# RMSNorm and projection on one core: warm-up matmuls on a tile of their own, and the last two stores from two engines

## The chip, the cores and the metric

The kernel runs on one core of a Trainium2 chip. The metric is the device time of one execution in microseconds (us), as the median of several runs. The span is what the profile shows of such a run, from the first to the last instruction; it is 1.7 to 1.9 us shorter than the device time. TensorE does the matmuls, VectorE (DVE) and ScalarE (ACT) the elementwise work, GpSimd (POOL) little, SyncE (SP) issues transfers. PSUM is the memory that the matmuls write to; an eviction copies a result out of it.

## The reference

```python
def reference(x, gamma, w_qkv, eps):          # x: 8 x 1024 x 768, w_qkv: 768 x 2304, float32
    rms = np.sqrt(np.mean(x ** 2, axis=-1, keepdims=True) + eps)
    x_norm = x / rms * gamma
    return np.matmul(x_norm, w_qkv).astype(np.float32)
```

The 8192 rows are 64 row tiles of 128 rows. The 768 columns of x are six blocks of 128 (the sums of the matmul), and the 2304 output columns are stored as 1024, 1024 and 256.

## The kernel before

The weights are scaled by gamma and rounded to bfloat16 once. Of each row tile, x is cast, transposed (by TensorE for the first four, by a transposing transfer for the others), multiplied with the weights, and scaled by 1/rms when PSUM is evicted. A plan gives each instruction a time, and the instructions are emitted in that order. TensorE starts with matmuls that produce nothing of use, to bring its clock up while the first data arrive.

```python
    ones = nc.const_aps.tensor(1.0, [P, NT], bf16)        # one constant per partition, repeated 512 times
    g6 = singles.tile([KO, P], f32)
    nc.scalar.dma_start(out=g6, in_=gamma.rearrange("(ko p) -> ko p", p=P))
    eps_sb = singles.tile([P, 1], f32)
    nc.vector.memset(eps_sb, float(eps))
    # ... identity, g_sb, w_b (the weights), then the pools of x, of weights and of outputs

    def idle(n, nl=P):
        wps = psum.tile([P, NT], f32, name="pm")
        for _ in range(n):
            nc.tensor.matmul(out=wps[:, :nl], lhsT=ones[:, :P], rhs=ones[:, :nl], start=True, stop=True)

    def store(t, h, n0, nl):
        p0 = PARTS[h][0]
        nc.sync.dma_start(out=of[t * P:(t + 1) * P, n0:n0 + nl], in_=OUT[t, h][:, n0 - p0:n0 - p0 + nl])

    def width(t, n0):             # the last row tile ends in two pieces of 128 columns
        return P if t == MT - 1 and n0 >= N - 2 * P else min(NT, N - n0)
    # ...
    at(0.0, idle, 5, NT)          # five warm-up matmuls
    at(2.8, gamma_in)             # gamma is transposed
    at(2.81, idle, 6, NT)         # six more, then the transposes of the first x tile
```

## Time and profile before

| what | value |
|---|---|
| device time, median of the first 3 runs | 388.34 us (388.09 to 388.74) |
| span of the profiled run | 386.9 us |
| TensorE busy | 98% of the span |
| warm-up matmuls on the constants | 14, 5.4 us busy |
| start of the last matmul to the end of the span | 3.88 us |

A line of the timeline reads: start, duration, engine, source line, operation, result and operands, shape and count; in brackets the idle time of the engine before it and what ended that. `PEld` is TensorE's weight load, `SPq` and `ACTq` are issues of transfers. The lines that carry the argument stand in the prediction below.

### The profile page before, as it was taken

Reading aid. Unit: us, or ns where it says so; the run is one execution under the profiler, and the core shown is the slowest. Engines: PE = TensorE matmul, PEld = TensorE weight load, DVE = VectorE, ACT = ScalarE, POOL = GpSimd, SP = SyncE. Lnnn points to the kernel's source line nnn. Section 1 sums busy time; section 2 is a strip of 40 time slices with the busy share of each in tenths; the row PEclk is TensorE's granted clock in tenths of the full one; section 3 lists DMA queues with packets and bytes.
Section 4 is the critical chain, followed back from the end, with each engine's and each line's share of the span. In section 5 each row is a group of like instructions: output and inputs, shape, how many; then the busy total and the mean of one; then the engine's idle time right before and its main releaser. Section 6 shows DMA issues by size and latency. Waiting matters only on the chain.

```text
span 386.9 us, 5470 instructions
## 1 busy us (share of the span) xinstructions
PE 379.9 (98%) x1927; PEld 192.2 (50%) x1965; DVE 153.4 (40%) x307; ACT 181.6 (47%) x365; POOL 6.5 (2%) x14
## 2 busy tenths in 40 slices
PE   8999999999999999999999999999999999999996
PEld 4444655454554554554554554554554554554553
DVE  2744534434333344333344333343333343333332
ACT  4752644453544443544444444544444534434532
POOL 0130000000000000000000000000000000000000
PEclk9999999999999999999999999999999999999999
DMA  8999999999999999999999999999999999999985
GB/s 291 390 281 402 398 318 363 344 338 283 351 297 308 303 295 321 293 300 322 305 289 313 285 318 312 293 309 275 326 311 297 304 317 305 304 306 289 292 264 186
DMA packets 89719, 119.91 MB, mean 310 GB/s; under 512 B 52438, under 2 KB 61532, under 8 KB 89692
## 3 DMA queue, kind: packets, MB, share of 16 engines
q1 hardware_dynamic: 89680, 119.56, 101.2%
q8 instruction: 15, 0.25, 0.3%
q14 instruction: 12, 0.10, 0.1%
q10 hardware_dynamic: 12, 0.00, 0.0%
HBM read 32.25 MB, written 75.50 MB: 279 GB/s over the span
## 4 chain that ended last, share of the span: by engine, by line
PE 89%; DMA 8%; issue 1%; DVE 1%; ACT 1%; SPq 0%
PE pm L235 89%; DMA x_t<-in_x_dram 3%; DMA w_f<-in_w_qkv_dram 2%; DMA xT<-xb 2%; DMA out_dram<-ot 1%; ACT ot L251 1%; DVE ot L249 0%; DVE xb L174 0%; SPq L160 0%; SPq L155 0%; SPq L255 0%; ACT w_b L168 0%
## 5 line engine op out<-in xcount | busy, mean ns | idle before, releaser
L235 PE MATMUL pm<-w_b,xT 128*128 128x512 bf16 (+1 forms) x1888 | 372.1, 357 | 2.1
L235 PEld LDWEIGHTS <-xT 128*128 128x128 bf16 x1926 | 187.9, 98 | 185.5 <-DMA xT<-xb 0.5
L249 DVE TENSOR_SCALAR ot<-pm,rstd 128x512 f32<-128x512 f32 (+1 forms) x161 | 111.5, 695 | 206.1 <-PE pm L235 201.7
L251 ACT ACTIVATE ot<-pm,rstd 128x512 f32<-128x512 f32 (+2 forms) x160 | 102.7, 643 | 191.7 <-PE pm L235 151.0
L185 ACT ACTIVATE sq<-x_t 128x768 bf16<-128x768 f32 x64 | 53.4, 834 | 3.0 <-DMA x_t<-in_x_dram 3.0
L174 DVE CAST xb<-x_t 128x768 bf16<-128x768 f32 x61 | 33.2, 545 | 13.6 <-DMA x_t<-in_x_dram 13.5
L187 ACT ACTIVATE rms<-ssq,eps_sb 128x1 f32<-128x1 f32 x64 | 18.8, 294 | 2.1
L185 ACT ACTIVATION_READ_ACCUMULATOR sq<-x_t 128x1 f32 x64 | 12.2, 191 | 0.0
L166 DVE TENSOR_SCALAR w_b<-w_f,g_sb 128x512 bf16<-128x512 f32 (+1 forms) x16 | 7.7, 499 | 5.9 <-DMA w_f<-in_w_qkv_dram 5.9
L192 DVE RECIPROCAL rstd<-rms 128x1 f32<-128x1 f32 x64 | 9.8, 153 | 0.0
L170 POOL TENSOR_SCALAR w_b<-w_f,g_sb 128x512 bf16<-128x512 f32 (+1 forms) x8 | 5.8, 735 | 23.5 <-DMA w_f<-in_w_qkv_dram 23.5
L284 PE MATMUL pm<-const-bfloat16-1.0 128*128 128x512 bf16 (+1 forms) x14 | 5.4, 539 | 0.8 <-PEq L340 0.8
L168 ACT ACTIVATE w_b<-w_f,g_sb 128x512 bf16<-128x512 f32 (+1 forms) x6 | 3.6, 612 | 2.7 <-DMA w_f<-in_w_qkv_dram 2.7
L212 PE MATMUL pm<-ident_f,x_t 128*128 128x128 f32 x18 | 2.8, 300 | 0.3 <-DMA x_t<-in_x_dram 0.3
L212 PEld LDWEIGHTS pm<-ident_f,x_t 128*128 128x128 f32 x18 | 2.4, 160 | 1.3 <-DMA x_t<-in_x_dram 0.9
L284 PEld LDWEIGHTS <-const-bfloat16-1.0 128*128 128x128 bf16 x14 | 1.5, 126 | 2.7 <-issue 2.7
L176 ACT CAST xT<-pm 128x256 bf16<-128x256 f32 (+1 forms) x5 | 2.3, 458 | 0.9 <-PE pm L212 0.7
L142 ACT ACT_TABLE_LOAD x1 | 1.3, 1283 | 1.4 <-PEq L340 1.4
L174 DVE CAST xT<-pm 128x512 bf16<-128x512 f32 x1 | 0.7, 691 | 1.4 <-PE pm L212 1.4
L267 DVE COPY g_sb<-pm 128x6 f32<-128x6 f32 x1 | 0.2, 164 | 1.9 <-PE pm L266 1.9
L266 PEld LDWEIGHTS pm<-ident_f,g 6*128 6x128 f32 x1 | 0.2, 177 | 1.0 <-issue 1.0
L174 DVE COPY xT<-pm 128x768 bf16<-128x768 bf16 x1 | 0.6, 557 | 0.0
(12 smaller groups left out, 2.5 us busy)
## 6 DMA issues: line engine op xcount, KB each, us to landing
out_dram<-ot SPq DMA_DIRECT2D x124, 512.0 KB, 3.9
x_t<-in_x_dram SPq DMA_DIRECT2D x64, 384.0 KB, 4.2
out_dram<-ot SPq DMA_DIRECT2D x63, 128.0 KB, 3.2
w_f<-in_w_qkv_dram SPq DMA_DIRECT2D x10, 512.0 KB, 7.4
out_dram<-ot SPq DMA_DIRECT2D x8, 256.0 KB, 2.0
w_f<-in_w_qkv_dram SPq DMA_DIRECT2D x4, 256.0 KB, 6.6
xT<-xb SPq DMA_TRANSPOSE x60, 4.3
w_f<-in_w_qkv_dram SPq DMA_DIRECT2D x2, 384.0 KB, 6.1
```

The source lines that it names most:

```text
L166: nc.vector.tensor_scalar(out=o, in0=i, scalar1=g, scalar2=None, op0=mult)
L168: nc.scalar.activation(out=o, in_=i, func=AF.Copy, scale=g, bias=0.0)
L170: nc.gpsimd.tensor_scalar(out=o, in0=i, scalar1=g, scalar2=1.0, op0=mult, op1=mult)
L174: nc.vector.tensor_copy(out=out, in_=in_)
L185: nc.scalar.activation(out=sq, in_=X[t], func=AF.Square, accum_out=ssq)
L187: nc.scalar.activation(out=rms, in_=ssq, func=AF.Sqrt, scale=inv_k, bias=eps_sb)
L192: nc.vector.reciprocal(out=r, in_=RS[t])
L212: nc.tensor.transpose(out=PT[t, h][:, ko - k0, :], in_=X[t][:, ko * P:(ko + 1) * P], identity=ident_f)
L235: nc.tensor.matmul(out=PM[t, n0][:, :nl], lhsT=XT[t][:, ko, :], rhs=w_b[:, ko, n0:n0 + nl], start=(b == 1), stop=(b == KO))
L249: nc.vector.tensor_scalar(out=o, in0=pm[:, :nl], scalar1=RS[t], scalar2=None, op0=mult)
L251: nc.scalar.activation(out=o, in_=pm[:, :nl], func=AF.Copy, scale=RS[t], bias=0.0)
L284: nc.tensor.matmul(out=wps[:, :nl], lhsT=ones[:, :P], rhs=ones[:, :nl], start=True, stop=True)
```

## The change

The warm-up gets a tile of its own in place of the program's constants; VectorE must write it first, and one warm-up matmul is given up for that time. At the end the second-to-last store is issued by ScalarE, so that the last one need not queue behind it on SyncE.

```diff
-    ones = nc.const_aps.tensor(1.0, [P, NT], bf16)
+    ones = singles.tile([P, NT], bf16)
+    nc.vector.memset(ones, 1.0)
...
     def store(t, h, n0, nl):
         p0 = PARTS[h][0]
-        nc.sync.dma_start(out=of[...], in_=OUT[t, h][...])
+        queue = nc.scalar if t == MT - 1 and n0 == N - 2 * P else nc.sync
+        queue.dma_start(out=of[...], in_=OUT[t, h][...])
...
-    at(0.0, idle, 5, NT)
+    at(0.0, idle, 4, NT)
```

More of the change, by code (lines that the diff above doesn't have):

```diff
@@ L254, in store @@
         p0 = PARTS[h][0]
-        nc.sync.dma_start(out=of[t * P:(t + 1) * P, n0:n0 + nl], in_=OUT[t, h][:, n0 - p0:n0 - p0 + nl])
+        queue = nc.scalar if t == MT - 1 and n0 == N - 2 * P else nc.sync
+        queue.dma_start(out=of[t * P:(t + 1) * P, n0:n0 + nl], in_=OUT[t, h][:, n0 - p0:n0 - p0 + nl])
     plan = []
```

## The prediction

> **What bounds the kernel now.** I read the page first: busy time by engine, the groups of instructions, the chain that ended last. Then the timeline of the first 14 us, the timeline of the last 4 us in narrow windows, and the DMA activity of those last microseconds, because the change touches only the two ends.
>
> ```profile
> PE 379.9 (98%) x1927; PEld 192.2 (50%) x1965; DVE 153.4 (40%) x307; ACT 181.6 (47%) x365; POOL 6.5 (2%) x14
> L235 PE MATMUL pm<-w_b,xT 128*128 128x512 bf16 (+1 forms) x1888 | 372.1, 357 | 2.1
> L284 PE MATMUL pm<-const-bfloat16-1.0 128*128 128x512 bf16 (+1 forms) x14 | 5.4, 539 | 0.8 <-PEq L340 0.8
> ```
>
> TensorE is busy 98% of the 386.9 us span, and its 1888 real matmuls sat idle only 2.1 us in all. That work is untouched, so the change can act only on the microseconds before the real work runs back to back and on the microseconds after the last matmul. The warm-up matmuls of the third line are what the first part edits.
>
> The start, from the timeline (start, duration, engine, line):
>
> ```profile
> 0.78 2.29 PE L284 MATMUL pm<-const-bfloat16-1.0 128*128 128x512 bf16 x5 [0.78 <-PEq L340]
> 0.81 0.06 DVE L139 MEMSET eps_sb<- 128x1 f32 x1 [0.81 <-PEq L340]
> 3.18 0.18 PEld L266 LDWEIGHTS pm<-ident_f,g 6*128 6x128 f32 x1 [1.02 <-issue]
> 3.38 2.74 PE L284 MATMUL pm<-const-bfloat16-1.0 128*128 128x512 bf16 x6
> 5.52 0.20 PEld L212 LDWEIGHTS pm<-ident_f,x_t 128*128 128x128 f32 x1 [0.31 <-DMA x_t<-in_x_dram]
> 5.91 1.14 PE L212 MATMUL pm<-ident_f,x_t 128*128 128x128 f32 x6
> 7.38 0.88 PE L212 MATMUL pm<-ident_f,x_t 128*128 128x128 f32 x6 [0.32 <-DMA x_t<-in_x_dram]
> ```
>
> The reader is to see two joints. TensorE runs five warm-up matmuls, the transpose of gamma, six more, then the transposes of the first x tile; and there is a gap at 7.38 us, where it waits 0.32 us for the second x tile from memory. From that tile on it runs almost without a gap. The gap is slack: whatever delays TensorE by less than about 0.3 us before it costs nothing.
>
> The end, from four narrow windows of the timeline, joined by dots:
>
> ```profile
> 382.56 1.02 DVE L249 TENSOR_SCALAR ot<-pm,rstd 128x512 f32<-128x512 f32 x2 [1.84 <-DMA out_dram<-ot]
> 382.90 0.37 ACT L251 ACTIVATE ot<-pm,rstd 128x128 f32<-128x128 f32 x1 [0.94 <-PE pm L235]
> 383.34 0.33 SPq L255 DMA_DIRECT2D out_dram<-ot  x1
> ...
> 383.77 0.88 SPq L255 DMA_DIRECT2D out_dram<-ot  x2
> ...
> 384.24 0.40 SPq L255 DMA_DIRECT2D out_dram<-ot  x1
> ```
>
> The last three stores stand in one queue on SyncE: the 256 KB one at 383.34, the second-to-last (64 KB, out of ScalarE's eviction) at 383.77, the last (64 KB, out of VectorE's) at 384.24. Both small evictions are done by 383.27 and 383.58, so the last store waits 0.66 us for its turn, not for data. It lands 1.6 us after its issue, and the span ends at 386.9.
>
> **What the Trainium skill says.** (1) "VectorE: DVE Perf Modes", section "Zero memsets can be issued as uint32 (trn2)": a memset takes one cycle per element whatever the dtype; the page's specification table gives 0.96 GHz. No memset of 512 elements is in the trace of before (the one of 1 element took 0.06 us), so nothing confirms it yet. (2) "TensorE: Matmul & The Clock Gate", "Part 1: The HAM clock gate": matmuls run at half clock until about 3.4 us of sustained activity has been seen in a window that runs freely. The trace agrees on the half clock, not on so short a wait: warm-up matmuls start 0.427 us apart, the first x tile's transposes 0.21 us apart up to 6.5 us, the second x tile's 0.11 us apart. The doubling falls near 6.6 us, 5.8 us after the first matmul. The profile's own clock row shows full clock throughout; the spacing decides. (3) "DMA: Bandwidth & Descriptors", "Issuing engines are not separate DMA queues": transfers issued from two engines run on the same 16 DMA engines, and only issue time is saved. The trace shows such issue time: 383.34 to 383.77 to 384.24 is 0.43 and 0.47 us a step.
>
> **The change part by part.** I also compared the instruction order of the two kernels on each engine. It changes in four places only: VectorE gets one memset, first of all; TensorE loses one warm-up load and matmul (the first group is 4, not 5) and its first load waits for VectorE; SyncE loses the second-to-last store; ScalarE gets it as its last instruction. All else stays in order.
>
> Start. The memset should last 512 / 0.96 GHz + 0.06 = 0.59 us (an estimate by page (1) and the small memset's 0.06 us). It starts at 0.81 and ends at 1.40; with 0.05 us for the semaphore (chosen from hand-overs elsewhere in the trace) the first matmul starts near 1.48 in place of 0.78: +0.70 us. One matmul fewer takes back 0.427. So the gamma transpose is at most 0.27 us later, and less if it waits for gamma's transfer: that one's last packets move between 2.6 and 2.8 us, and a wait event stands at 3.1. The x transposes then start at 5.91 to 6.18, and six of them at the cold 0.21 us spacing occupy TensorE until at most 6.18 + 1.28 = 7.46, against the 7.38 where the second tile arrives. If the clock doubles at 6.6 as before they are done by 7.0. Loss: 0.0 to 0.1 us. The moment of doubling can itself move later, as activity starts 0.7 us later; transposes and matmuls after 7.38 that are still cold cost half of the cold time, and I allow 0.1 us on average. VectorE's identity cast and eps move by up to 0.6 us; the cast's first reader comes at 11.98, the scaled weights wait for a transfer at 4.62: hidden. Sum of the start: +0.1 us.
>
> End. SyncE issues the 256 KB store at 383.34 and then the last store at 383.77 in place of 384.24: 0.47 us earlier. ScalarE issues the second-to-last at about 383.3, right after its own eviction. If nothing else limited, the end would move by 0.47. But the three transfers share the 16 engines: from the first data packet at 384.14 to the last near 385.45 these are already about 75% busy, and 96% between 384.5 and 385. Packed without gaps the same work is 0.75 x 1.31 = 0.98 us, ending near 385.15, 0.3 us earlier at best. I take 0.2: some of the gap goes, since the last 64 KB no longer trails behind its issue. Sum of the end: -0.2 us. Total: 388.34 + 0.1 - 0.2 = 388.2 us.
>
> **The rivals.** First, the transfers bind: the last packet lands when it did, because the same bytes pass the same engines, and two queues issuing at once slow each other. For it: the 96%. Against it: 25% gaps. Time: 388.4. Second, issue binds wholly: the full 0.47 us comes off and the start costs nothing: 387.9. Third, the late start hits: the clock doubles one window (3.4 us by page (2)) later, so that up to 3 us of work beyond 7.38 runs at half rate; cost up to 1.5 us, time up to 389.7. For it: in before the doubling came late, so the phase matters. Against it: only a start delay of 0.7 of a 3.4 us window, so about one run in five, and the median hides it. Fourth, a new wait at the end: ScalarE's store uses another completion semaphore, whose earlier user is eight transfers back and has long landed; nothing to wait for.
>
> **Range and chances.** The runs of before spread from 388.09 to 388.74. With an end gain of 0 to 0.47 and a start cost of 0 to 0.5, the median should lie from 387.8 to 388.7, eight times in ten. Two per cent is 7.8 us; the whole stretch before 7.38 and after the last matmul is about 11 us, and nothing in the change removes or doubles most of it. Within 2%: 0.985; slower 0.01 (cold clock for long, or a wait unseen); faster 0.005.
>
> **What would show each step right or wrong.** The memset of the ones tile: 0.5 to 0.6 us on VectorE, first matmul near 1.48 us (a memset of 0.2 us would mean a fast mode, start near 1.1). The gamma transpose between 3.2 and 3.5. The second x tile's transposes still at 7.4, released by the transfer. The transpose spacing there 0.11 us, not 0.21. At the end: ScalarE's issue beside SyncE's of the 256 KB store, the last SyncE issue about 0.43 us after the one before, the last matmul at its old time within 0.2 us, and the span after the last matmul (now 383.2 to 386.9, 3.7 us) shortened to about 3.5. Wrong would be a shift of the last matmul, which would mean that the start passes through to the end, or a last landing that does not move although its issue did.

## The result, and the profile after

The changed kernel took 389.12 us (six runs, 388.59 to 389.52), the kernel before, in six runs of the same rounds, 388.27 us (388.09 to 388.74). The ratio is 1.0020, with a 95% interval of 1.0007 to 1.0033. A ratio here is the mean time of one kernel's fast runs over that of the other's of the same rounds, so it is not quite the ratio of the medians. By the 2% rule this is the same; but it is 0.85 us slower, every run of the one above nearly every run of the other, and outside the range of 387.8 to 388.7. The profiled run of before was its slowest (388.74), that of the changed kernel an ordinary one (389.14), so the two traces differ by 0.47 us of span and show only about half of the difference.

The start of the changed kernel, from its timeline:

```profile
0.91 0.48 DVE L136 MEMSET ones<- 128x512 bf16 x1 [0.91 <-PEq L343]
1.46 1.89 PE L287 MATMUL pm<-ones 128*128 128x512 bf16 x4 [1.46 <-DVE eps_sb L140]
3.27 0.18 PEld L269 LDWEIGHTS pm<-ident_f,g 6*128 6x128 f32 x1 [0.84 <-issue]
3.47 2.74 PE L287 MATMUL pm<-ones 128*128 128x512 bf16 x6
6.01 1.02 PE L213 MATMUL pm<-ident_f,x_t 128*128 128x128 f32 x6
7.70 0.87 PE L213 MATMUL pm<-ident_f,x_t 128*128 128x128 f32 x6 [0.67 <-DMA x_t<-in_x_dram]
```

The first matmul is at 1.46 us, as forecast; the first x tile's transposes start at 6.01, 0.10 us later than before, also within the forecast. But the second x tile now arrives in time for 7.70, not 7.38, and TensorE waits 0.67 us for it. Nothing in the change touches that transfer: SyncE issues it at the same time in both traces. So 0.32 us of the difference between these two traces come from a transfer.

A little more is added at the next place where TensorE waits for a transfer, the row tile that is transposed on its way. The two lines are of the kernel before and of the changed one:

```profile
28.99 2.06 PEld L235 LDWEIGHTS <-xT 128*128 128x128 bf16 x11 [0.55 <-DMA xT<-xb]
```
```profile
29.42 1.62 PEld L236 LDWEIGHTS <-xT 128*128 128x128 bf16 x9 [0.68 <-DMA xT<-xb]
```

The step from 28.99 to 29.42 is 0.43 us, and the last matmul starts 0.43 us later too (383.41 against 382.98). From 29 us on the two kernels keep pace.

The end of the changed kernel, from two windows of the timeline:

```profile
383.00 1.02 DVE L250 TENSOR_SCALAR ot<-pm,rstd 128x512 f32<-128x512 f32 x2 [1.84 <-PE pm L236]
383.33 0.37 ACT L252 ACTIVATE ot<-pm,rstd 128x128 f32<-128x128 f32 x1 [0.94 <-PE pm L236]
383.73 0.40 ACTq L258 DMA_DIRECT2D out_dram<-ot  x1
383.78 0.33 SPq L258 DMA_DIRECT2D out_dram<-ot  x1
...
384.20 0.38 SPq L258 DMA_DIRECT2D out_dram<-ot  x1
```

The issues do what was meant: ScalarE's at 383.73, SyncE's large one beside it, the last 0.42 us after that and not 0.90 us. Yet the end did not come closer. What SyncE waits for at the end, of the kernel before and of the changed one (us in total, times, longest):

```profile
SPq L354 <- DMA out_dram<-ot: 1.1, 1, 1.1
```
```profile
SPq L357 <- DMA out_dram<-ot: 1.7, 1, 1.7
```

The time saved in issuing is spent waiting for the landing. From the start of the last matmul to the end of the span it is 3.88 us before and 3.92 us after.

### The profile page after: what moved, and what is told of

Read it like the earlier page. It is cut to its first block, busy times and chain, and to the rows that moved or that the text cites. A ratio compares the mean times of both kernels' runs of the same rounds, so it can differ in the third digit from the quotient of the medians.

```text
span 387.3 us, 5507 instructions
## 1 busy us (share of the span) xinstructions
PE 381.3 (98%) x1964; PEld 191.9 (50%) x1964; DVE 153.7 (40%) x308; ACT 181.5 (47%) x365; POOL 6.6 (2%) x14
## 4 chain that ended last, share of the span: by engine, by line
PE 91%; DMA 7%; DVE 0%; issue 0%; SPq 0%; ACT 0%
PE pm L236 91%; DMA x_t<-in_x_dram 3%; DMA w_f<-in_w_qkv_dram 2%; DMA xT<-xb 2%; DVE ot L250 0%; ACT ot L252 0%; DVE xb L175 0%; SPq L161 0%; SPq L156 0%; ACT w_b L169 0%
## 5 line engine op out<-in xcount | busy, mean ns | idle before, releaser
L236 PE MATMUL pm<-w_b,xT 128*128 128x512 bf16 (+2 forms) x1926 | 374.1, 357 | 0.2 <-DMA xT<-xb 0.2
L287 PE MATMUL pm<-ones 128*128 128x512 bf16 (+1 forms) x13 | 5.0, 533 | 1.5 <-DVE eps_sb L140 1.5
L287 PEld LDWEIGHTS <-ones 128*128 128x128 bf16 x13 | 1.4, 126 | 3.1 <-issue 1.7
```

What stands on the lines that cost most here:

```text
L236: nc.tensor.matmul(out=PM[t, n0][:, :nl], lhsT=XT[t][:, ko, :], rhs=w_b[:, ko, n0:n0 + nl], start=(b == 1), stop=(b == KO))
```

## The experiments

Eighteen kernels ran in five sessions, each session on one chip, and all gave correct results. "Before" in the table is the median of the kernel before, which runs in every session as the common yardstick. e5 to e8 and e9 to e12 ran on the same chip, and nine of the ten yardstick runs of e9 to e12 are those of e5 to e8.

| run | median (lowest to highest), us | before | ratio (95%) |
|---|---|---|---|
| e1_ones_only | 388.43 (388.31 to 388.86) | 388.30 | 1.0002 (0.9989 to 1.0015) |
| e2_store_only | 388.34 (388.08 to 389.38) | 388.30 | 1.0003 (0.9991 to 1.0015) |
| e3_before_again | 388.13 (388.00 to 389.68) | 388.30 | 1.0006 (0.9991 to 1.0021) |
| e4_after_again | 388.43 (388.32 to 390.90) | 388.30 | 1.0015 (0.9996 to 1.0033) |
| e5_unread_tile | 388.32 (388.04 to 388.88) | 388.43 | 0.9996 (0.9983 to 1.0008) |
| e6_late_start | 388.42 (388.30 to 389.26) | 388.43 | 1.0001 (0.9987 to 1.0015) |
| e7_one_column | 387.86 (387.69 to 388.47) | 388.43 | 0.9987 (0.9974 to 0.9999) |
| e8_own_early | 388.36 (388.17 to 388.51) | 388.43 | 0.9996 (0.9984 to 1.0009) |
| e9_split_tail | 388.34 (388.01 to 388.88) | 388.40 | 0.9997 (0.9984 to 1.0009) |
| e10_after_third | 388.58 (388.42 to 388.71) | 388.40 | 1.0002 (0.9988 to 1.0015) |
| e11_after_short | 388.44 (388.31 to 388.83) | 388.40 | 1.0000 (0.9986 to 1.0013) |
| e12_before_third | 388.44 (388.25 to 388.50) | 388.40 | 0.9997 (0.9984 to 1.0011) |
| e13_small_and_split | 387.46 (387.30 to 388.38) | 388.35 | 0.9981 (0.9968 to 0.9994) |
| e14_one_column_again | 387.90 (387.68 to 388.35) | 388.35 | 0.9988 (0.9976 to 1.0000) |
| e15_after_fourth | 388.90 (388.47 to 390.29) | 388.35 | 1.0022 (1.0007 to 1.0036) |
| e16_before_fourth | 388.63 (388.20 to 389.41) | 388.35 | 1.0007 (0.9995 to 1.0019) |
| e17_before_pad | 387.94 (387.58 to 388.01) | 388.42 | 0.9985 (0.9971 to 0.9999) |
| e18_after_pad | 388.27 (387.81 to 388.94) | 388.42 | 0.9995 (0.9983 to 1.0008) |

### Each part alone, and both kernels again

The first theories were that the start (A) or the second store queue (B) carries the loss. e1 has the first and third hunk of the diff alone, e2 the second alone; e3 and e4 are the two kernels unchanged, to see what repeats.

> The first part alone (own ones tile, four warm-up matmuls in the first group), stores as before. Theory A, the start carries the loss: +0.6 to +0.9 us over before (ratio 1.0015 to 1.0023), second x tile late or clock late, tail of 3.7 us after the last matmul. Theory B, the second store queue carries the loss: within 0.2 us of before (ratio 0.9995 to 1.0005).

> The second part alone (the second-to-last store by ScalarE), warm-up as before. Theory A, the start carries the loss: within 0.2 us of before, and the time from last matmul to the end of the span stays at 3.7 us because the three transfers bind. Theory B, the second queue carries the loss: +0.6 to +0.9 us, seen as a longer wait of SyncE for the last landing.

> The kernel before once more, as a control: ratio 1.000 within 0.0006, and a second trace of it. If the second x tile reaches TensorE at 7.35 us again, the 7.67 of the changed kernel belongs to the change; if it comes anywhere between 7.3 and 7.8, that difference between the two traces is chance.

> The changed kernel once more: ratio 1.0015 to 1.0025 and a second trace of it. If the loss is that of the start, the last matmul ends 0.3 us or more later than in before; tail 3.7 us. The spread of its runs (0.9 us in the first six) should come back if a free-running clock window is behind it, and shrink to 0.3 us if it was chance.

Neither part alone shows the 0.6 to 0.9 us that theory A or B asked for: 0.13 us for the start and 0.04 us for the store, both within the scatter. The changed kernel itself came out 0.13 us above before at the median, with single runs up to 390.90. The copy of the kernel before also had two runs of six above 389.6. So the first comparison's 0.85 us is not what one gets each time.

The traces say what moves. The completion of a transfer is recorded for each of the sixteen DMA engines that carry it. In e3 and e2 the second x tile is whole at 6.60 and 6.53 us. In the first trace of before fifteen parts of it had landed by 6.45 us and one came at 7.33; in the changed kernel that last part came at 7.65, in e1 at 7.44, in e4 at 8.32. **The gap at 7.38 us that the prediction took for fixed slack was one late sixteenth of a transfer.** Of all twenty traces four show such late parts, one of each kernel in the first comparison, and e1 and e4; the other sixteen have the tile whole between 6.53 and 6.96 us.

e2 settles the end. In the seven traces with the second queue the time from the start of the last matmul to the end of the span is 3.91 to 3.92 us, and in the eleven with the old stores 3.88 to 3.89 us. The second queue costs 0.03 us. The packets show where its gain went: from the first data packet of the last three stores to the last it takes 1.33 us before and 1.28 us after, for the same 384 KB on the same sixteen engines, although the last issue came 0.47 us earlier. The last landing then follows the last packet by 0.45 us in place of 0.36. Why it is later was not tried; a second queue by itself is not the reason, since in e13, below, which has one too, it is 0.35 us.

### Late start, streaming, or place

Three candidates remained for a loss at the start: TensorE begins later (A), the wide tile is streamed while x arrives (B), or the tile's place or VectorE's half microsecond matters (C).

```diff
 # e5_unread_tile: before, plus a tile that is written and never read
+    own = singles.tile([P, NT], bf16)
+    nc.vector.memset(own, 1.0)
 # e6_late_start: the first part of the change, but the moving operand from the constants
-  lhsT=ones[:, :P], rhs=ones[:, :nl]
+  lhsT=ones[:, :P], rhs=cols[:, :nl]          # cols: the constants
 # e7_one_column: before, with
+    one = singles.tile([P, 1], bf16)
+    nc.vector.memset(one, 1.0)
+    ones = one.to_broadcast([P, NT])
 # e8_own_early: before, with a tile of 128 columns, streamed four times over
```

> The kernel before with the own tile allocated and written by VectorE, but never read: five warm-up matmuls on the constants from 0.78 us. Theory A, the loss is the late start of TensorE: median as before, within 0.15 us, best runs near 388.0. Theory C, the loss comes of the tile's place or of VectorE's half microsecond (later identity and eps, other addresses): +0.3 to +0.4 us in median and best run.

> The weights of the warm-up from the own tile, so that TensorE starts near 1.45 us with four matmuls as in the change, but the moving operand from the constants. Theory A, late start: +0.3 to +0.4 us over before in median and best run, as with the change. Theory B, the loss comes of streaming the own tile's 512 columns (memory traffic beside the arriving x tile): within 0.15 us of before, second x tile landing near 6.6 us.

> An own tile of one column, repeated, with five warm-up matmuls: the memset lasts 0.06 us and TensorE starts near 0.95 us. Theory A, late start: within 0.15 us of before. Theory B, streaming: within 0.15 us of before too, as nothing is streamed from a wide tile.

> An own tile of 128 columns, streamed four times over, five warm-up matmuls: memset about 0.2 us, TensorE starts near 1.1 us and the gamma transpose at 3.3 us, as in the change. Theory A, late start, judged by the first matmul: +0.1 us. Theory A in its narrower form, the end of the warm-up queue near 6.0 us counts: +0.3 us. Theory B, streaming: +0.3 to +0.4 us.

At the median none of e5, e6 and e8 differs from before by more than 0.11 us, and e8, which streams its tile, has no late part of x. B, and C in this form, are not supported; A, which asked for 0.3 to 0.4 us in e6, is not visible in these medians. e7 did what none of the theories said: 0.57 us faster than before, though its TensorE starts later. That needed an explanation of its own, below.

### Where the late start goes

e10 and e12 are the two kernels once more on one chip; e11 shortens the second warm-up group of the changed kernel.

```diff
 # e11_after_short
-    at(2.81, idle, 6, NT)
+    at(2.81, idle, 5, NT)
```

> The changed kernel a third time. Theory A, the late start of TensorE passes through to the end: median +0.3 us or more over before in every session, best run not below 388.3. Theory D, TensorE waits for the second x tile in any case, and the differences between sessions come of transfers that stall by chance: median within 0.2 us of before, with single runs 0.5 to 2 us late as in either kernel.

> The changed kernel with five warm-up matmuls in the second group in place of six: the x transposes could start 0.43 us earlier. Theory A: 0.3 to 0.4 us faster than the changed kernel. Theory D: no difference beyond 0.15 us in the undisturbed runs, the second x tile's landing (6.5 to 7.7 us) still releases TensorE.

> The kernel before a third time, control: ratio 1.000 within 0.001. Its trace: the second x tile's last sixteenth lands between 6.5 and 7.4 us, and the span less that landing is 379.6 us as in its other traces (386.9 less 7.33, 386.2 less 6.60).

These traces have no late part: the second tile is whole at 6.83 (e12), 6.77 (e10) and 6.74 us (e11). TensorE in e12, the kernel before (second warm-up group, twelve transposes of two x tiles, first real matmuls):

```profile
3.20 2.09 PE L284 MATMUL pm<-const-bfloat16-1.0 128*128 128x512 bf16 x6
5.89 1.86 PE L212 MATMUL pm<-ident_f,x_t 128*128 128x128 f32 x12 [0.61 <-DMA x_t<-in_x_dram]
7.59 0.59 PE L235 MATMUL pm<-w_b,xT 128*128 128x512 bf16 x2
```

In e10, the changed kernel:

```profile
3.57 2.74 PE L287 MATMUL pm<-ones 128*128 128x512 bf16 x6
6.10 1.95 PE L213 MATMUL pm<-ident_f,x_t 128*128 128x128 f32 x12
7.95 0.60 PE L236 MATMUL pm<-w_b,xT 128*128 128x512 bf16 x2
```

In e11, the changed kernel with one warm-up matmul fewer:

```profile
3.48 2.31 PE L287 MATMUL pm<-ones 128*128 128x512 bf16 x5
5.80 1.87 PE L213 MATMUL pm<-ident_f,x_t 128*128 128x128 f32 x12
7.50 0.59 PE L236 MATMUL pm<-w_b,xT 128*128 128x512 bf16 x2
```

In e12 the transposes wait for the first tile, and the first real matmul comes 0.76 us after the second tile is whole. In the undisturbed traces of the changed kernel this step is 1.18 us (e10), 1.35 us (e15) and 1.28 us (e18, below, with one more small tile).

What goes with it is the clock. Near the start of each trace the spacing of TensorE's starts halves (from 0.21 to 0.11 us between transposes): the clock doubles. The table has the undisturbed traces in which this came late, and e8. In the nine others the clock doubles between 4.0 and 6.0 us, and the step is 0.75 to 0.76 us.

| trace | first matmul, us | clock doubles, us | transposes start, us | second tile whole to first real matmul, us |
|---|---|---|---|---|
| e8_own_early | 1.05 | 5.6 | 6.03 | 0.76 |
| e11_after_short | 1.45 | 6.3 | 5.80 | 0.76 |
| e13_small_and_split | 0.93 | 6.5 | 5.91 | 0.88 |
| e6_late_start | 1.45 | 6.9 | 6.02 | 0.90 |
| e10_after_third | 1.46 | 7.1 | 6.10 | 1.18 |
| e18_after_pad | 1.45 | 7.2 | 6.01 | 1.28 |
| e15_after_fourth | 1.45 | 7.5 | 6.00 | 1.35 |

In e8 the transposes start nearly as late as in e10, but at the doubled clock, and nothing is lost:

```profile
6.03 1.85 PE L213 MATMUL pm<-ident_f,x_t 128*128 128x128 f32 x12
7.72 0.59 PE L236 MATMUL pm<-w_b,xT 128*128 128x512 bf16 x2
```

**So what costs is not the late start alone, but a late start with a clock that doubles late.** In the three undisturbed traces of the changed kernel it doubled only at 7.1 to 7.5 us; transposes at half clock were not done when the second tile was whole, and the first real matmul came 0.42 to 0.59 us later. From the first matmul to the doubling it takes 3.2 us (e2) to 6.0 us (e15), and it varies between traces of the same kernel (4.2 to 6.0 us in those of the changed one). A start 0.68 us later makes a late doubling likelier: it came after 6.5 us in four of the eight traces whose first matmul is near 1.45 us, and in two of the twelve others. No run varied the start without the clock. In e11 the step is 0.76 us again, but there the clock doubled at 6.3 us, so it is not shown that the shorter warm-up is the reason.

But the loss does not all reach the end. The next wait for a transposed tile, in e10 and in e11:

```profile
28.59 2.49 PEld L236 LDWEIGHTS <-xT 128*128 128x128 bf16 x13 [0.37 <-DMA xT<-xb]
```
```profile
28.61 2.27 PEld L236 LDWEIGHTS <-xT 128*128 128x128 bf16 x12 [0.70 <-DMA xT<-xb]
```

e11 began 0.45 us earlier and resumes at the same 28.6 us; it only waits 0.33 us longer. e12 resumes at 28.53. Theory A's 0.3 to 0.4 us for e11 was a miss: its median is 0.14 us under that of e10. The transfers set the pace up to here, and in these traces most of the loss at the start is hidden behind them.

e9 tests the end. The last row tile's 512 columns before the two small pieces become two pieces of 256, each stored when it is evicted.

```diff
 # e9_split_tail
-    for n0 in [*range(0, N, NT)] + [N - P] * (t == MT - 1):
+    last = [0, NT, 2 * NT, 3 * NT, 3 * NT + 2 * P, N - 2 * P, N - P]
+    for n0 in last if t == MT - 1 else range(0, N, NT):
```

> The start of before; the last row tile's 512 columns ahead of the two small pieces are cut in two pieces of 256, each stored when it is evicted, all by SyncE. Theory T, the bytes still to be moved after the last eviction set the tail: at the last store only 64 KB and what is left of the one before are to move, so the time from the last matmul to the end falls from 3.7 us to 3.0 to 3.3 us, and the median by 0.4 to 0.7 us. Theory U, issue and fixed latency set the tail: 3.7 us as before, or more for the extra store.

The tail, in the measure used above, went from 3.88 to 3.68 us: bytes moved earlier do shorten it, but by 0.20 us, less than expected. Four stores now stand close together on SyncE, and the last is issued at 383.77, 0.39 us after its data were ready. The median, expected 0.4 to 0.7 us under before, is 0.06 us under it.

### Side by side again, the narrow tile again, and a better end

e15, e16 and e14 repeat kernels. e13 joins the one-column tile, the split, and a last store by ScalarE, which has just evicted those columns.

```diff
 # e13_small_and_split: e7_one_column and e9_split_tail, and
+    queue = nc.scalar if t == MT - 1 and n0 == N - P else nc.sync
```

> The changed kernel a fourth time, beside the kernel before. Theory D, chance stalls at the start: median 0.1 to 0.3 us over before, single runs up to 2 us late, no repeat of the +0.85 us of the first comparison. Theory E, the wide own tile makes stalls more frequent: +0.5 us or more again, and a trace whose second x tile has one or more of its sixteen parts landing after 7.2 us.

> The kernel before a fourth time, on the same chip as the fourth run of the changed kernel: ratio 1.000 within 0.001. Theory D: stalled runs occur here as often as in the changed kernel. Theory E: no more than one run in six is over 388.9.

> The own tile of one column, again: its first test ran 0.57 us under before at the median, which neither theory of the start explains (its TensorE starts 0.15 us later than before). If that was chance: within 0.2 us of before. If it is real: 0.4 to 0.6 us faster again.

> The own tile of one column, the last 512 wide piece in two pieces, and the very last store by ScalarE, which has just evicted it. Split alone shortened the tail by 0.20 us, with its last store issued 0.39 us after its eviction, behind two others. Theory T, bytes and then issue: the last issue comes at once, the time from the start of the last matmul to the end falls from 3.88 to 3.3 to 3.5 us, and the median is 0.3 to 0.5 us under before, more if the one-column tile gains by itself. Theory U, fixed latency: 3.7 us as with the split alone.

The changed kernel is 0.55 us over before in its session, and 0.27 us over e16, the copy of before that ran in the same way. So the first sign of theory E (0.5 us or more) came true against the yardstick; the second, a late part of the second x tile, did not (whole at 6.69 us). The profiled run of e15 was slow for a reason far from both ends. Two lines of its timeline, the issue of a transposing transfer and the matmuls that need it:

```profile
67.48 2.27 SPq L222 DMA_TRANSPOSE xT<-xb  x1
...
75.04 1.25 PE L236 MATMUL pm<-w_b,xT 128*128 128x512 bf16 x5 [1.49 <-DMA xT<-xb]
```

The transfer takes 7.5 us and TensorE stands still for 1.49 us. The kernel before has the same wait, 0.3 us in e16. By its place in time it falls on the first row tile that the plan loads without its extra 6 us of lead; that this is why it has nothing to spare was not tried.

e14 is 0.45 us faster than before, so the narrow tile's gain repeats. e13 is 0.89 us faster at the median, ratio 0.9981, and beats both kernels. Its end, from two windows:

```profile
382.73 0.37 ACT L255 ACTIVATE ot<-pm,rstd 128x128 f32<-128x128 f32 x1 [0.20 <-PE pm L239]
382.99 0.40 SPq L260 DMA_DIRECT2D out_dram<-ot  x1
...
383.13 0.38 ACTq L260 DMA_DIRECT2D out_dram<-ot  x1
```

The last store is issued 0.03 us after its eviction, and from the start of the last matmul to the end it is 3.43 us, within what was expected: 0.20 us for the bytes that had gone earlier, 0.25 us for the queue. Here, with the bytes out of the way, a second queue helped.

### The place of the tiles

e7's tile takes 32 bytes per partition (each small tile does, in the built program) and stands first, so all later tiles move up by 32 bytes. The weight buffers and x tiles stood 224 bytes past a multiple of 256 before, and on a multiple of 256 in e7. The wide tile of the change (1024 bytes), the unread tile of e5 and the tile of e8 (256 bytes) leave them at 224. e17 and e18 add such a small tile to the two kernels and read it nowhere.

```diff
 # e17_before_pad (on before), e18_after_pad (on the changed kernel)
+    pad = singles.tile([P, 1], f32)
+    nc.vector.memset(pad, 0.0)
```

> The kernel before with one more small tile (32 bytes per partition), written once by VectorE and never read, so that every large tile behind it stands 32 bytes higher, on a multiple of 64 bytes in place of 32 past one; nothing else changes. Theory P, the gain of the one-column tile is that of the place: 0.4 to 0.6 us under before, as e7 and e14, and 2 KB packets of 84 ns in place of 85 to 86. Theory Q, the gain belongs to the warm-up operand: within 0.15 us of before.

> The changed kernel with the same small tile: its wide tile of 1024 bytes left the places at 32 past a multiple of 64, the small one moves them onto it. Theory P: 0.4 to 0.6 us under the changed kernel, that is at or a little under before; what it stands above the padded before is what the change itself costs, by theory D 0.1 to 0.3 us, by theory E (more stalls with a wide tile) 0.5 us or more. Theory Q: as the changed kernel, 0.1 to 0.6 us over before.

Theory P holds: the padded before is 0.48 us under before, and the padded change 0.15 us under it (the changed kernel without the pad did not run in that session). The expectation speaks of multiples of 64; the same 32 bytes also reach a multiple of 256, and the runs do not tell the two apart. The stretch from 8 to 28 us, in which transfers set the pace (the last two columns are DMA share and GB/s), of e12 (before), e17 and e18:

```profile
8.00:28.00 20.00, 19.71 (x100) 9.33 (x102) 11.82 (x26) 13.27 (x28) 5.37 (x7) 1.00 1.09 351
```
```profile
8.00:28.00 20.00, 19.89 (x102) 9.34 (x102) 12.29 (x27) 13.73 (x29) 5.26 (x7) 1.00 1.06 363
```
```profile
8.00:28.00 20.00, 19.89 (x102) 9.56 (x103) 11.89 (x27) 13.71 (x29) 5.38 (x7) 1.00 1.09 365
```

363 and 365 GB/s stand against 351; all five traces with the new places have 361 to 365, all fifteen with the old ones 331 to 352. What this saves is a wait: in all fifteen TensorE's weight load waits for a transposing transfer between 28 and 32 us (0.2 to 1.8 us), in the five it does not; three of them wait near 23 us, for at most 0.35 us. The 3072 packets of 2 KB in the first 40 us, all of them weights, take 84 ns at the median and at the 90th percentile in e7, e13, e14, e17 and e18; in the fifteen traces with the old places they take 84 to 86 ns at the median and 94 to 95 at the 90th percentile. The Trainium skill's "DMA: Bandwidth & Descriptors", section "How a descriptor splits into AXI transactions", says that a descriptor which does not start on a multiple of 256 bytes costs a transaction more, with an example that begins at byte 224. The runs agree in direction. But the section explains it for a transaction that reads, and here the places that moved are those that the transfers write; that this is the mechanism is not shown.

With the new places the wait near 28 us, behind which e10 hid its loss, is gone. The second tile is whole at 6.65 us in both; e17 and then e18:

```profile
5.75 1.82 PE L214 MATMUL pm<-ident_f,x_t 128*128 128x128 f32 x12
7.41 0.59 PE L237 MATMUL pm<-w_b,xT 128*128 128x512 bf16 x2
```
```profile
6.01 2.09 PE L215 MATMUL pm<-ident_f,x_t 128*128 128x128 f32 x12
7.93 0.59 PE L238 MATMUL pm<-w_b,xT 128*128 128x512 bf16 x2
```

The first real matmul is 0.52 us later (the clock doubles at 5.3 us in e17, at 7.2 us in e18), and the median is 0.33 us higher (388.27 against 387.94).

**What the change costs.** Four pairs ran alike on one chip each: e4 and e3, e10 and e12, e15 and e16, e18 and e17. The changed one is above the other by 0.30, 0.14, 0.27 and 0.33 us at the medians. The sign is the same four times, but the runs of each pair overlap, so 0.1 to 0.3 us is an estimate of what the change itself costs. Of this 0.03 us is the end. The rest fits the late start where the clock doubles late, as in the traces of e10, e15 and e18 (not in that of e4, where it doubled at 5.6 us and a stalled transfer hid the start). That link is argued from the traces, not timed by itself. **Open:** the remaining half microsecond or more of the first comparison. Stalled transfers, at the second x tile, near 28 to 31 us and near 73 to 75 us, move single runs of either kernel by 0.3 to 2 us. Runs over 389.0 us are 8 of 23 for the changed kernel, 3 of 15 for the copies of before, and 1 of 47 for before as the common yardstick. These counts do not settle whether the change makes stalls more frequent: the two for the kernel before differ strongly from each other, and the four other kernels with the late start (e1, e6, e11, e18) have 2 of 19.

## Why the prediction was wrong, point by point

- **The memset and the first matmul:** 0.48 us and 1.46 us against 0.59 and 1.48. The gamma transpose at 3.27 us, within 3.2 to 3.5. Right.
- **"The gap is slack: whatever delays TensorE by less than about 0.3 us before it costs nothing."** This step failed, and with it the +0.1 us for the start. The gap was one stalled sixteenth of the second x tile in that one trace; where nothing stalls, the tile is whole at 6.5 to 7.0 us. Whether TensorE is done by then hangs on the clock. The prediction named that risk, but took the moment of doubling from one trace (6.6 us) and allowed 0.1 us for a later one. In the undisturbed traces of the changed kernel it came at 7.1 to 7.5 us, and the first real matmul 0.42 to 0.59 us later, of which a wait near 28 us hides a part. In the trace of the first comparison it came at 6.4 us and the first tile's transposes were done at 7.03 us, as forecast; there the 0.32 us came from the stalled transfer.
- **"Sum of the end: -0.2 us."** The sign was wrong: +0.03 us, in seven traces against eleven. The estimate packed the same work without gaps; the packets did close up by 0.05 us, and the last landing came 0.09 us later after them. The gaps were also read too large: 75% is the share of a window that begins at 383.9 us, before the first packet, while the profile's DMA share from 384.14 to 385.45 us is 87%. By the prediction's own way of reckoning that leaves 0.17 us to gain (an estimate), not 0.3. The first rival, that the transfers bind, was right. Of what the prediction asked to see, the issue of ScalarE beside SyncE's was there, and both signs of being wrong came: the last matmul moved (by 0.43 us in the first comparison), and the time from it to the end did not shrink although the last issue came earlier.
- **The range.** With +0.3 us for the change the centre would have been 388.6 us, near the edge of the range. The rest to 389.12 us is chance or unexplained. The range took the scatter of three runs of before (0.65 us) for the scatter of the kernel, though the traces show three places (the second x tile, near 28 us, near 73 us) where TensorE waits for a transfer, and each stalled by a microsecond or more in some trace.
- **"Slower by over 2%" and "faster by over 2%"** were rightly given almost nothing. The third rival, a clock that doubles late, is the mechanism that the traces show at the start, in a milder form: at most 7.5 us and 0.59 us lost at the first real matmul, against the 1.5 us that it allowed. The prediction took it for one run in five; among the traces that start late it doubled after 6.5 us in four of eight.

## What to carry to other kernels

A gap in one trace is slack only if what ends it is fixed: look at the sixteen completions of the transfer behind it, or at a second trace, before you lean on it. Read the moment at which the clock doubles from several traces, since it differs between runs of one program. A second queue for the last stores gained nothing here while the bytes already queued took longer than the issue that was saved; try first to move bytes earlier, then to part the queues. When a small new tile changes the time of a kernel that waits for transfers, check where it has moved all the other tiles.

## What the Trainium skill lacked or had wrong

- "VectorE: DVE Perf Modes", "Zero memsets can be issued as uint32 (trn2)", with 0.96 GHz in its specifications: one cycle per element would be 0.53 us for 512 elements. The memset took 0.48 us in all, with its fixed part; 128 elements took 0.17 us and one 0.06 us.
- "TensorE: Matmul & The Clock Gate", "Part 1: The HAM clock gate": its remark that the moment varies from run to run holds, but it has it around 4 us and varying by half a microsecond. Here the doubling came between 3.2 us (e2) and 6.0 us (e15) after the first matmul.
- "DMA: Bandwidth & Descriptors", "How a descriptor splits into AXI transactions": the section does not say what misplaced buffers cost in time. Here a shift of 32 bytes per partition was worth 0.45 to 0.57 us of 388, and the stretch bound by transfers ran at 361 to 365 GB/s in place of 331 to 352.
- No page has how the time from the last packet to the last landing changes with the engines that issue the last stores: 0.35 to 0.36 us with one queue, 0.44 to 0.45 us with the second-to-last store on ScalarE, but 0.35 us in e13 with the last one there.
